# Two output products of a DiT layer: activations stationary, gates as rows, no transposition at the residual

## The chip, the core and the metric

The kernel runs on one core of one Trainium2 chip. The metric is the device time of one launch in microseconds (us). The kernel before took 1759.86 us in the median of three runs (1759.07 to 1762.25).

## The reference

The program computes two layers of a diffusion transformer on 512 latent tokens and 256 context tokens, 1024 channels wide, in f32. The change touches the first layer's two residual updates:

```python
a = rms_norm(h, norm1_g) * (1 + sc1) + sh1          # sc, sh, g: adaLN, from c
y = concat([y_conv, y_na], -1) @ w_out              # even mixer: convolution, neighbourhood attention
h = h + g1 * y                                      # g1: one gate per channel
t = rms_norm(h, norm2_g) * (1 + sc2) + sh2
h = h + g2 * ((silu(t @ w1) * (t @ w3)) @ w2)       # D_FF = 2816
# the same for the context tokens, with gates of their own
```

After them comes the second layer: an odd mixer (window attention and differential attention), and a mixture of eight experts. It is not touched.

## The kernel before, in words

All 768 tokens lie in `h` as six tiles of 128 tokens (partitions) by 1024 channels, f32: tiles 0 to 3 are the latents, 4 and 5 the context. Products are done in f16 with each f32 operand split in two (hi and lo) and three products for each 128 rows of the contraction: hi·hi, hi·lo, lo·hi. Activations for a product lie transposed, channels on partitions (`yT`, `gT`, `aT`), in both halves.

Weights are streamed by `Stream`: a block of up to 1 MB goes by DMA to one of two staging slots (`wst`), ACT casts the hi half (L282), DVE computes the lo half (L283). Two blocks are fetched ahead. Between the weight blocks lie the blocks `adr` of the adaLN matrix of later steps; each costs DVE four multiply-and-sum instructions of 128x1024 (L384, `adjk`).

The output projection of the first mixer (in `layer0`, L1042 to L1070, tiles `eops`) uses `mm1`: the weights of 128 output channels (one of eight `d`) are stationary, 512 columns of latent tokens (part 0) or 256 of context (part 1) move past. So the result is transposed, channels on partitions, and `resid` (L468) brings it back: ACT evicts it and multiplies by the gate, which is one number per partition (L474, `yT`), TensorE transposes it in 128x128 pieces, four in part 0 and two in part 1 (L477, `ytp`), DVE adds it to `h` (L479). After d = 4, 6 and 7 ACT sums the squares of what has been added (L465). The second product of the feed-forward (`ffn`, tiles `f` from `gT`, 22 contraction steps) is built in the same way, and also stores the four latent tiles of `h` to DRAM (`h_spill`, L1135).

Both products are followed by an RMS norm (`norm_steps`), one for the latents and one for the context. It sums the partial squares (L488), takes a reciprocal square root in small DVE steps (L330 to L342), scales the rows (L430 on DVE, L428 on ACT, tile `n`, or `h` in place), and then takes eight steps, one for each 128 channels: four transposes on PE (L440, `nps`), scale and shift on ACT (L447, `af`), hi and lo halves on DVE (L452, L453). The steps of the latents' norm are put between the matmuls of the last part 1, as many to a `d` as `NSTEP1` and `NSTEP2` say; the product that follows (`f` from `yT` after the projection, `pscq` after the feed-forward) needs them. The Tile framework sets the order of the instructions on each engine; each engine runs its queue in order.

`mm2` (L354) is the other form of a product, used in the next layer: 128 tokens of activations are stationary, up to 512 columns of weights move, and the result has tokens on partitions.

Of the kernel before, what the change touches and what calls it, by code (L numbers as in the profile page):

```python
# [50 lines left out]
NSTEP1 = (0, 2, 3, 3)  # L51
NSTEP2 = ((), (), (1, 3, 5, 7, 9), (0, 2, 4))
# [17 lines left out]
SSQ = {4: (0, 0), 6: (1, 5), 7: (2, 7)}  # L70

# [59 lines left out]
def layouts(i):  # L131
# [18 lines left out]
    A['w_evo'] = _pairs(_m1(f('ev_w_out')[0]))  # L150
    t1, t3 = _m1(f('ffn_w1')[0]), _m1(f('ffn_w3')[0])
    A['w_f13'] = _pairs(np.stack([t1, t3], 1).reshape(44, 128, 8, 128))
    A['w_f2'] = _w2(f('ffn_w2')[0])
# [161 lines left out]
class K:  # L315
# [168 lines left out]

    def ssq_sum(self, pool, ssq, part):
        t0, nt, mc = PARTS[part]
        ss = self.small.tile([128, nt], F32, name="sst", tag=f"sst{nt}", bufs=2)
        self.nc.vector.tensor_reduce(out=ss, in_=ssq[:, t0:t0 + nt, :], axis=AX.X, op=OP.add)  # L488
        return ss


    def blocks(self):
# [53 lines left out]
    def setup(self, ctx):  # L546
# [22 lines left out]
        self.adab = [cols[:, 0:48], cols[:, 48:96]]  # L569
        self.ada_o = ada_order()  # L570
# [371 lines left out]
    def conv_gemm(self, a, yT, cp, pp):  # L942
# [25 lines left out]
        for c in range(0, 4, 2):  # L968
# [29 lines left out]
            w = block()  # L998
            for ci in range(2):
# [11 lines left out]
    def layer0(self):  # L1011
# [30 lines left out]
        with ExitStack() as c:  # L1042
            rp = c.enter_context(tc.tile_pool(name="ro0", bufs=1))
            pp = c.enter_context(tc.tile_pool(name="po0", bufs=1, space=PSUM))
            def gemm(w, d, part):
                s0, sn = CHUNKS[part]
                ps = pp.tile([128, 512], F32, name=f"eops{d}_{part}", tag="m", bufs=4)
                for k in range(KD):
                    self.mm1(ps, w[0][:, d % 2], w[1][:, d % 2], k, yT[:, 0, :, s0:s0 + sn], yT[:, 1, :, s0:s0 + sn],
                             [(0, sn)], k == 0, k == 7)  # L1050
                self.resid(d, part, ps, 0, rp, pp, "tp", ssq=self.ssq)

            self.ssq = self.small.tile([128, 6, 3], F32, name="ssq1", tag="ssq", bufs=2)
            norm = None
            for d0 in (0, 2, 4):
                ws = []
                for j in ((d0 // 2,) if d0 < 4 else (2, 3)):
                    w = self.S.get(('evo', j))
                    ws.append([z.rearrange("p (j k c) -> p j k c", j=2, k=8) for z in w])
                for part in range(2):  # L1060
                    for d in range(d0, d0 + 2 * len(ws)):
                        if norm is None and d0 == 4 and part == 1:

                            norm = self.norm_steps(1, 0, self.h, self.ssq, yT, rp, pp, "n")
                            next(norm)
                        gemm(ws[(d - d0) // 2], d, part)
                        for _ in range(NSTEP1[d - 4] if norm is not None else 0):
                            next(norm, None)
            for _ in norm:
# [4 lines left out]
    def ffn(self):  # L1074
        nc, tc = self.nc, self.tc
        a = self.a1
        with ExitStack() as c:
# [25 lines left out]
            self.ssq = self.small.tile([128, 6, 3], F32, name="ssq2", tag="ssq", bufs=2)  # L1103
            self.hd = self.dram.tile([4, 128, D], F32, name="h_spill")
            for ds in ((0,), (1,), (2,), (3,), (4,), (5,), (6, 7)):
                ws = [[z.rearrange("p (k c) -> p k c", k=11) for z in self.S.get(('f2', 2 * d + s))]
                      for d in ds for s in range(2)]
                if ds == (6, 7):
                    self.spill(0, 6)
                for part, (s0, sn) in enumerate(CHUNKS):  # L1110
                    if ds == (6, 7) and part:

                        self.spill(6, 8)
                        a = self.a2 = self.big.tile([128, 2, KD, NT], F16, name="aT2", tag="A")
                        norm = self.norm_steps(2, 0, self.h, self.ssq, a, fp, pp, "ad", natural=True, inplace=True, aftag="gf")
                        next(norm)
                    for d in ds:
                        ps = pp.tile([128, 512], F32, name=f"f2_{d}_{part}", tag="m", bufs=6)
                        for s in range(2):
                            wh, wl = ws[2 * (d - ds[0]) + s]  # L1120
                            for k in range(11):
                                self.mm1(ps, wh, wl, k, gT[:, 0, :, s0:s0 + sn], gT[:, 1, :, s0:s0 + sn], [(0, sn)],
                                         s == 0 and k == 0, s == 1 and k == 10, kk=11 * s + k)
                                if ds == (6, 7) and part and k in NSTEP2[2 * (d - 6) + s]:
                                    next(norm, None)
# [1019 lines left out]
```

## Time and profile before

| | |
|---|---|
| median of the runs | 1759.86 us |
| profiled execution, own time | 1761.97 us |
| its span | 1760.1 us |
| its mean granted TensorE clock | 0.983 |
| output projection, first `eops` to first `f` matmul | 310.92 to 388.33 us |
| feed-forward's first product | 388.33 to 735.92 us |
| feed-forward's second product, to first `pscq` matmul | 735.92 to 925.06 us |

The profile is of one execution; its times stand in microseconds from the start of the span. PE is TensorE, PEld its weight loads, DVE is VectorE, ACT is ScalarE. A group's line gives line number, engine, operation, output and inputs with shapes, and the count; a busy PE counts the whole pipeline depth of each matmul, so the distance from one start to the next (the pitch) is what a stream of them costs, not their duration.

### The profile page before, as it was taken

To read this page: it belongs to the slowest core of one execution; us is meant where nothing else is said; L and a number is where in the kernel's file an instruction comes from. 1 tells how busy PE (TensorE), PEld (TensorE's weight loads), DVE (VectorE), ACT (ScalarE), POOL (GpSimd) and SP (SyncE) were. 2 spreads that over 40 slices of the span, in tenths; PEclk is the share of its full clock that TensorE was granted. 3 is DMA by queue.
4 is the path that set the end of the run, shared out by engine and by line. 5 is a ranking of instruction groups with operands and counts; after the bars stand their busy time and mean duration, and the time that the engine had idled before them with its cause. 6 is when DMAs were issued, how large, how long until landed. Compare 5 with 4: busy or idle time off the path is not lost. (4 is left out here: it accounts for less than half of the span.)

```text
span 1760.1 us, 36123 instructions
## 1 busy us (share of the span) xinstructions
PE 1651.1 (94%) x15124; PEld 1160.4 (66%) x15124; DVE 1235.6 (70%) x2388; ACT 887.5 (50%) x1436; POOL 141.3 (8%) x100
## 2 busy tenths in 40 slices
PE   4999999999999999999998999988789999999996
PEld 2455566556556666566555466457689988999996
DVE  7775989777654544333148999696797688788883
ACT  7754554253222221111244667564666577786773
POOL 0000000000000000000000000352130001010211
PEclk9999999999999999999999999999889999999998
DMA  8412432633443332233312201112658889999892
GB/s 340 149 63 100 156 109 97 243 117 120 144 144 137 127 144 97 74 114 114 117 61 81 96 1 61 44 43 77 232 179 314 258 281 359 337 338 359 301 327 65
DMA packets 53736, 286.83 MB, mean 163 GB/s; under 512 B 7760, under 2 KB 12880, under 8 KB 29504
## 3 DMA queue, kind: packets, MB, share of 16 engines
q1 hardware_dynamic: 47472, 272.78, 42.8%
q0 software_dynamic: 5232, 10.96, 2.9%
q8 instruction: 120, 1.97, 0.4%
q10 hardware_dynamic: 864, 0.72, 0.1%
q14 instruction: 48, 0.39, 0.1%
HBM read 272.57 MB, written 11.08 MB: 161 GB/s over the span
## 5 line engine op out<-in xcount | busy, mean ns | idle before, releaser
L351 PEld LDWEIGHTS <-whi 128*128 128x128 f16 x5120 | 464.5, 98 | 185.4 <-issue 11.5
L351 PE MATMUL f<-yT,whi 128*128 128x512 f16 (+1 forms) x1408 | 326.8, 327 | 1.5 <-ACT af L447 1.5
L351 PEld LDWEIGHTS <-wlo 128*128 128x128 f16 x2560 | 251.5, 98 | 90.0 <-issue 2.6
L283 DVE SCALAR_TENSOR_TENSOR wlo<-wst,whi 128x2048 f16<-128x2048 f32 (+2 forms) x134 | 214.6, 1612 | 60.4 <-ACT whi L282 60.3
L351 PE MATMUL f<-yT,wlo 128*128 128x512 f16 (+1 forms) x704 | 229.9, 327 | 0.0
L282 ACT ACTIVATE whi<-wst 128x2048 f16<-128x2048 f32 (+2 forms) x134 | 179.1, 1354 | 99.9 <-PE f L351 72.0
L384 DVE SCALAR_TENSOR_TENSOR adjk<-wst,srow 128x1024 bf16<-128x1024 f32 x96 | 117.3, 1222 | 98.0 <-DMA wst<-in_w_adr_dram 97.0
L351 PE MATMUL f<-gT,whi 128*128 128x512 f16 (+1 forms) x704 | 164.4, 326 | 0.0
L351 PEld LDWEIGHTS <-aT 128*128 128x128 f16 x2376 | 153.7, 98 | 2.9 <-issue 2.4
L351 PE MATMUL mps<-xT,whi 128*128 128x176 f16 (+6 forms) x1408 | 141.1, 227 | 1.1 <-DVE xT L1871 0.7
L351 PE MATMUL mps<-xT,wlo 128*128 128x176 f16 (+6 forms) x704 | 135.7, 227 | 0.0
L351 PE MATMUL f<-gT,wlo 128*128 128x512 f16 (+1 forms) x352 | 114.7, 326 | 0.0
L351 PE MATMUL mps<-xT,aT 128*128 128x112 f16 (+6 forms) x1584 | 105.8, 225 | 0.2 <-issue 0.2
L479 DVE TENSOR_TENSOR h<-h,ytp 128x256 f32<-128x256 f32 (+1 forms) x48 | 24.3, 506 | 112.1 <-PE ytp L477 111.8
L351 PE MATMUL cvps<-aT,whi 128*128 128x512 f16 (+1 forms) x384 | 84.0, 332 | 2.8 <-ACT Kl L646 2.3
L1101 ACT CAST gT<-g 128x512 f16<-128x512 f32 (+1 forms) x23 | 14.0, 608 | 130.8 <-DVE g L1098 130.8
L351 PE MATMUL mps<-mgT,whi 128*128 128x176 f16 (+6 forms) x704 | 72.1, 227 | 1.4 <-DVE mgf L1890 0.9
L351 PE MATMUL mps<-mgT,wlo 128*128 128x176 f16 (+6 forms) x352 | 68.2, 227 | 0.0
L1096 ACT ACTIVATE s<-f 128x512 f32<-128x512 f32 (+1 forms) x44 | 21.5, 489 | 84.0 <-PE f L351 83.9
L358 PEld LDWEIGHTS <-aT 128*128 128x128 f16 x384 | 37.4, 99 | 39.4 <-DVE aT L453 6.5
L351 PE MATMUL eops<-yT,whi 128*128 128x512 f16 (+1 forms) x256 | 61.2, 326 | 1.1 <-DVE yc L1002 1.1
L1098 DVE SCALAR_TENSOR_TENSOR g<-f,s 128x512 f32<-128x512 f32 (+1 forms) x44 | 24.4, 556 | 52.3 <-PE f L351 52.3
(420 smaller groups left out, 3470.8 us busy)
## 6 DMA issues: line engine op xcount, KB each, us to landing
wst<-in_w_adr_dram SPq DMA_DIRECT2D x32, 1024.0 KB, 4.8
wst<-in_w_m_dram SPq DMA_DIRECT2D x26, 1024.0 KB, 6.3
Kd<-in_w_m_dram SPq DMA_DIRECT2D x25, 1024.0 KB, 8.3
h<-in_w_m_dram SPq DMA_DIRECT2D x24, 1024.0 KB, 10.1
wst<-in_w_f_dram SPq DMA_DIRECT2D x22, 1024.0 KB, 4.9
Kd<-in_w_m_dram SPq DMA_DIRECT2D x19, 704.0 KB, 5.8
Qc<-in_w_m_dram SPq DMA_DIRECT2D x13, 1024.0 KB, 6.3
wst<-in_w_m_dram SPq DMA_DIRECT2D x18, 704.0 KB, 6.5
```

What stands on the lines that cost most here:

```text
L282: nc.scalar.activation(h, x, AF.Copy, scale=self.scale)
L283: nc.vector.scalar_tensor_tensor(out=l, in0=x, scalar=SW, in1=h, op0=OP.mult, op1=OP.subtract)
L351: mm(ps[:, s0:s0 + sn], w[:, k, :], a[:, kk, s0:s0 + sn], start=first and p == 0, stop=last and p == 2)
L358: mm(ps, al[:, kk, t0:t0 + 128], wh[:, k, :], start=False, stop=last)
L384: nc.vector.scalar_tensor_tensor(out=jk, in0=st[:, j * D:(j + 1) * D], scalar=1.0, in1=self.srow[:, t, :], op0=OP.mult, op1=OP.mult, accum ...
L479: nc.vector.tensor_tensor(out=hs, in0=hs, in1=tp[:, 0:w].rearrange("p (t c) -> p t c", t=nt), op=OP.add)
L1096: nc.scalar.activation(s[:, 0:sn], p[0][:, 0:sn], AF.Silu, scale=DESC)
L1098: nc.vector.scalar_tensor_tensor(out=g[:, 0:sn], in0=p[1][:, 0:sn], scalar=DESC * SA, in1=s[:, 0:sn], op0=OP.mult, op1=OP.mult)
L1101: nc.any.tensor_copy(gh, g[:, 0:sn])
```

## The change

Both products change to the form of `mm2`. The 1024 output channels are done in two halves of 512; in each half the six token tiles t come in turn, with 128 tokens stationary and 512 columns of weights moving. The result has tokens on partitions, as `h` has, and `resid_rows` needs no transposition: DVE multiplies the PSUM tile by the gates, adds the product to `h`, and ACT sums the squares of each half tile. A gate is now a number per column, so it is wanted as a row on all partitions: `gate_send` transposes the gates on TensorE and stores them to DRAM once per product, `gate_rows` reads a half of them to 128 partitions by DMA (`grow`, 128x2x512, one buffer). The weights of both products are laid out anew by halves; the second product of the feed-forward has 12 blocks in place of 16. Steps of the latents' norm stand after every second contraction step of the last two token tiles of half 1. The spill is four DMAs of half a tile's channels after t = 3 of each half.

```diff
--- before.py
+++ after.py
@@ -69,6 +67,8 @@
 PARTS = [(0, 4, 0), (4, 2, 1), (0, 2, 0), (2, 2, 0)]
 SSQ = {4: (0, 0), 6: (1, 5), 7: (2, 7)}
 
+F2K = (3, 3, 4, 4, 4, 4)
+
 
 
 def _perm():
@@ -482,6 +489,35 @@
             for t in range(t0, t0 + nt):
                 self.sumsq(pool, self.h, ssq[:, t, c:c + 1], t, c0 * 128, (dt + 1) * 128)
 
+    def gate_send(self, gi, pool, pspool, tag, bufs=2):
+
+        nc = self.nc
+        tp = pspool.tile([128, 512], F32, name=f"gtp{gi}", tag=tag, bufs=bufs)
+        gc = pool.tile([128, 16], F32, name="gc16", tag="gc16", bufs=1)
+        nc.vector.tensor_copy(gc.rearrange("p (t k) -> p t k", t=2), self.gate[gi].rearrange("p k t -> p t k"))
+        nc.tensor.transpose(tp[0:16, 0:128], gc, self.ident)
+        r = pool.tile([16, 128], F32, name="grow16", tag="grow16", bufs=1)
+        nc.vector.tensor_copy(r, tp[0:16, 0:128])
+        self.gd[gi] = self.dram.tile([16, 128], F32, name=f"gate_d{gi}")
+        nc.sync.dma_start(out=self.gd[gi], in_=r)
+
+    def gate_rows(self, gi, half, pool):
+
+        g = pool.tile([128, 2, 512], F32, name=f"grow{gi}_{half}", tag="grow", bufs=1)
+        v = self.gd[gi].rearrange("a c -> (a c)")
+        src = bass.AP(tensor=v.tensor, offset=v.offset + 512 * half, ap=[[0, 128], [D, 2], [1, 512]])
+        self.nc.sync.dma_start(out=g, in_=src)
+        return g
+
+    def resid_rows(self, t, half, ps, g, pool, ssq, tag="yT", bufs=2):
+
+        V = self.nc.vector
+        c = slice(512 * half, 512 * half + 512)
+        y = pool.tile([128, 512], F32, name=f"yg{t}_{half}", tag=tag, bufs=bufs)
+        V.tensor_tensor(out=y, in0=ps, in1=g[:, t // 4, :], op=OP.mult)
+        V.tensor_tensor(out=self.h[:, t, c], in0=self.h[:, t, c], in1=y, op=OP.add)
+        self.sumsq(pool, self.h, ssq[:, t, half:half + 1], t, 512 * half, 512 * half + 512)
+
     def ssq_sum(self, pool, ssq, part):
         t0, nt, mc = PARTS[part]
         ss = self.small.tile([128, nt], F32, name="sst", tag=f"sst{nt}", bufs=2)
@@ -515,8 +551,10 @@
             add(('cv', j), 'w_cv', j)
             for b in range(8 + 2 * j, min(10 + 2 * j, ADV)):
                 ada(0, b)
+        def rows(key, name, half, k0, n):
+            o.append((key, A[name][half][:, 512 * k0:512 * (k0 + n)], 512 * n))
         for j in range(4):
-            add(('evo', j), 'w_evo', j)
+            rows(('evo', j), 'w_evo', j // 2, 4 * (j % 2), 4)
             ada(0, ADV + j)
         rest = [(0, b) for b in range(20, 24)] + [(1, b) for b in range(24)]
         n = 0
@@ -996,6 +1035,8 @@
                     post.pop(0)()
                     yield 0.8
             w = block()
+            if c:
+                self.gate_send(0, cp, pp, "PT")
             for ci in range(2):
                 ps = yield from gemm(w, ci)
                 yc = cp.tile([128, NT], F32, name="yc", tag="yc", bufs=1)
@@ -1042,30 +1083,22 @@
         with ExitStack() as c:
             rp = c.enter_context(tc.tile_pool(name="ro0", bufs=1))
             pp = c.enter_context(tc.tile_pool(name="po0", bufs=1, space=PSUM))
...
+            self.ssq = self.small.tile([128, 6, 3], F32, name="ssq1", tag="ssq", bufs=2)[:, :, 0:2]
             norm = None
...
+            for half in range(2):
+                grow = self.gate_rows(0, half, rp)
+                ws = [[z.rearrange("p (k c) -> p k c", k=4) for z in self.S.get(('evo', 2 * half + j))] for j in range(2)]
+                for t in range(6):
+                    if half and t == 4:
+
+                        norm = self.norm_steps(1, 0, self.h, self.ssq, yT, rp, pp, "n")
+                        next(norm)
+                    ps = pp.tile([128, 512], F32, name=f"eops{half}_{t}", tag="m", bufs=4)
+                    for k in range(KD):
+                        self.mm2(ps, *ws[k // 4], k % 4, yT[:, 0], yT[:, 1], k, t * 128, k == 0, k == 7)
+                        if norm is not None and k % 2:
                             next(norm, None)
+                    self.resid_rows(t, half, ps, grow, rp, self.ssq)
             for _ in norm:
                 pass
         self.dump('h1', self.h)
@@ -1082,6 +1115,8 @@
             next(norm)
             for f in range(22):
                 w = [z.rearrange("p (j k c) -> p j k c", j=2, k=8) for z in self.S.get(('f13', f))]
+                if f == 6:
+                    self.gate_send(1, fp, pp, "ad")
                 for part, (s0, sn) in enumerate(CHUNKS):
                     p = []
                     for i in range(2):
@@ -1100,30 +1135,39 @@
                     gh, gl = (gT[:, z, f, s0:s0 + sn] for z in range(2))
                     nc.any.tensor_copy(gh, g[:, 0:sn])
                     nc.vector.tensor_tensor(out=gl, in0=g[:, 0:sn], in1=gh, op=OP.subtract)
...
+            self.ssq = self.small.tile([128, 6, 3], F32, name="ssq2", tag="ssq", bufs=2)[:, :, 0:2]
             self.hd = self.dram.tile([4, 128, D], F32, name="h_spill")
...
+            norm = None
+            for half in range(2):
+                grow = self.gate_rows(1, half, fp)
+                ps = [pp.tile([128, 512], F32, name=f"f2_{half}_{t}", tag="m", bufs=6) for t in range(6)]
+
+                def gemm(t, ws):
+                    for w, k0, n in ws:
+                        for k in range(n):
+                            kk = k0 + k
+                            self.mm2(ps[t], *w, k, gT[:, 0], gT[:, 1], kk, t * 128, kk == 0, kk == 21)
+                            if norm is not None and kk % 2:
+                                next(norm, None)
+                    if ws[-1][1] + ws[-1][2] == 22:
+                        self.resid_rows(t, half, ps[t], grow, fp, self.ssq, "s", 3)
+                        if t == 3:
+                            self.spill(4 * half, 4 * half + 4)
+                k0, ws = 0, []
+                for j, n in enumerate(F2K):
+                    w = [z.rearrange("p (k c) -> p k c", k=n) for z in self.S.get(('f2', 6 * half + j))]
+                    ws.append((w, k0, n))
+                    k0 += n
+
+                    if j == 4:
+                        continue
+                    for t in range(6):
+                        if half and j == 5 and t == 4:
+                            a = self.a2 = self.big.tile([128, 2, KD, NT], F16, name="aT2", tag="A")
+                            norm = self.norm_steps(2, 0, self.h, self.ssq, a, fp, pp, "ad", natural=True, inplace=True, aftag="gf")
+                            next(norm)
+                        gemm(t, ws)
+                    ws = []
             for _ in norm:
                 pass
         self.dump('h2', self.h)
```

DVE's queue at the end of the output projection, before: `ytp_7_0` is the last transposed result of the latents, `ssq` and `sst` the sums of squares, `rs_*` the reciprocal square root, `n_0` the normalised tile.

```order
L479 TENSOR_TENSOR h<-h,ytp_7_0_4388 128x4x128 [waits PE_49]
L488 TENSOR_REDUCE sst<-ssq_3906 128x4 [waits Activation_49]
L330 TENSOR_SCALAR rs_v<-sst 128x4 [waits DVE_49]
L331 TENSOR_SCALAR rs_r<-rs_v 128x4 [waits DVE_49]
L340 TENSOR_TENSOR rs_t<-rs_r 128x4 [waits DVE_49]
L341 SCALAR_TENSOR_TENSOR rs_t<-rs_t,rs_v 128x4 [waits DVE_49]
L479 TENSOR_TENSOR h<-h,ytp_4_1_4450 128x2x128 [waits PE_49]
L342 SCALAR_TENSOR_TENSOR rs_r<-rs_t,rs_r 128x4 [waits DVE_49]
```

And now: `yg_1` is the product with the gates of half 1, `eops_3` and `eops_4` the results of token tiles 3 and 4, `adjk` the adaLN instructions.

```order
L517 TENSOR_TENSOR yg_1_4297<-eops_3_4272,grow_1_4139 128x512 [waits PE_49]
L518 TENSOR_TENSOR h<-h,yg_1_4297 128x512 [waits DVE_49]
L391 SCALAR_TENSOR_TENSOR adjk,adred<-wst_4496,srow 128x1024 [waits DMAHW1_49]
L524 TENSOR_REDUCE sst<-ssq_3914 128x4 [waits Activation_49]
L391 SCALAR_TENSOR_TENSOR adjk,adred<-wst_4496,srow 128x1024 [waits DVE_49]
L337 TENSOR_SCALAR rs_v<-sst 128x4 [waits DVE_49]
L391 SCALAR_TENSOR_TENSOR adjk,adred<-wst_4496,srow 128x1024 [waits DVE_49]
L338 TENSOR_SCALAR rs_r<-rs_v 128x4 [waits DVE_49]
L517 TENSOR_TENSOR yg_1_4384<-eops_4_4323,grow_1_4139 128x512 [waits PE_49]
L347 TENSOR_TENSOR rs_t<-rs_r 128x4 [waits DVE_49]
L391 SCALAR_TENSOR_TENSOR adjk,adred<-wst_4496,srow 128x1024
L348 SCALAR_TENSOR_TENSOR rs_t<-rs_t,rs_v 128x4 [waits DVE_49]
```

Four `adjk` instructions and the multiplication for tile 4 now stand in the chain from the last addition of the latents to `n_0`; before, only one addition of a context piece stood there.

PE's queue where the latents' norm begins, before: `eops_1` tiles are of part 1 (context), `nps` are the norm's transposes.

```order
L351 LDWEIGHTS whi_4071
L351 MATMUL eops_1_4507<-yT_1586,whi_4071 128x256
L351 LDWEIGHTS wlo_4072
L351 MATMUL eops_1_4507<-yT_1586,wlo_4072 128x256
L351 LDWEIGHTS whi_4071
L351 MATMUL eops_1_4507<-yT_1586,whi_4071 128x256
L440 MATMUL nps_0_4489<-ident,n_0_4418 128x128 [waits DVE_49]
L440 MATMUL nps_1_4498<-ident,n_0_4418 128x128
L351 LDWEIGHTS whi_4071
L351 MATMUL eops_1_4507<-yT_1586,whi_4071 128x256
L351 LDWEIGHTS wlo_4072
L351 MATMUL eops_1_4507<-yT_1586,wlo_4072 128x256
```

And now, in token tile 5 of half 1, the last of the projection:

```order
L365 LDWEIGHTS yT_1586
L365 MATMUL eops_5_4389<-whi_3953,yT_1586 128x512
L447 MATMUL nps_0_4330<-ident,n_0_4318 128x128 [waits DVE_49]
L447 MATMUL nps_1_4345<-ident,n_0_4318 128x128
L363 LDWEIGHTS yT_1586
L363 MATMUL eops_5_4389<-whi_3953,yT_1586 128x512
L364 LDWEIGHTS yT_1586
L364 MATMUL eops_5_4389<-wlo_3954,yT_1586 128x512
L447 MATMUL nps_0_4330<-ident,n_0_4318 128x128 [waits DVE_49]
L447 MATMUL nps_0_4330<-ident,n_0_4318 128x128 [waits Activation_49]
L447 MATMUL nps_1_4345<-ident,n_0_4318 128x128 x2
L365 LDWEIGHTS yT_1586
```

Before, the first `nps` came after four matmuls of d = 6's part 1, with 44 of 256 columns still to come; now it comes in tile 5, after seven of its eight contraction steps, with three of 512 columns still to come.

SP's queue at the projection's start, now: `gate_d` is the store of the gates, `grow_0` the rows of half 0, `wst` blocks of weights and of adaLN, `h` the loads of the residual.

```order
L266 DMA wst_3603<-in_w_adr_dram 128x2048 [waits DMAHW6_49,DMAHW5_49,DVE_49]
L266 DMA wst_3609<-in_w_evo_dram 128x2048 [waits DMAHW4_49,DVE_49]
L502 DMA gate_d_3617<-grow_3615 16x128 [waits DMAHW0_49,DVE_49]
L509 DMA grow_0_3915<-gate_d_3617 128x2x512 [waits DMAHW0_49,PE_49]
L266 DMA wst_3930<-in_w_adr_dram 128x2048 [waits DMAHW6_49,DVE_49]
L1082 DMA h<-in_x_dram 128x1024 [waits PE_49]
L1082 DMA h<-in_x_dram 128x1024 x3
```

The two new DMAs stand ahead of an adaLN block and of the six loads of `h`, which followed directly upon the third weight block and that adaLN block before.

## Rows read from the trace of the kernel before

**Rows 1.** Part 1 of the page: busy time, share, instructions of each engine.
```profile
PE 1651.1 (94%) x15124; PEld 1160.4 (66%) x15124; DVE 1235.6 (70%) x2388; ACT 887.5 (50%) x1436; POOL 141.3 (8%) x100
```

**Rows 2.** Windows: start:end, length, busy time by engine, PEclk, DMA share, GB/s.
```profile
310.92:388.33 77.41, 74.68 (x464) 45.52 (x464) 57.41 (x116) 34.64 (x70) 0.00 (x0) 1.00 0.48 179
388.33:395.20 6.87, 6.87 (x25) 2.79 (x25) 6.87 (x19) 1.27 (x4) 0.00 (x0) 0.75 0.63 229
395.20:735.92 340.72, 340.56 (x2105) 205.78 (x2104) 180.63 (x346) 79.01 (x97) 0.00 (x0) 1.00 0.36 126
735.92:925.06 189.14, 184.56 (x1139) 110.98 (x1137) 60.27 (x103) 50.54 (x87) 0.00 (x0) 1.00 0.28 98
```

**Rows 3.** PE's timeline in the next stage, whose activations are stationary.
```profile
928.11 0.38 PE L358 MATMUL pscq<-whi,aT 128*128 128x512 f16 x1
...
930.91 0.38 PE L356 MATMUL pscq<-whi,aT 128*128 128x512 f16 x1
```

**Rows 4.** PE's timeline about a set of transposes: start, length, instruction, count.
```profile
368.99 0.38 PE L351 MATMUL eops<-yT,whi 128*128 128x256 f16 x2
...
369.65 0.27 PE L351 MATMUL eops<-yT,whi 128*128 128x256 f16 x1
369.94 0.66 PE L477 MATMUL ytp<-ident,yT 128*128 128x128 f32 x4
370.43 0.27 PE L351 MATMUL eops<-yT,whi 128*128 128x256 f16 x1
```

**Rows 5.** Line groups in 310.92:388.33: shapes, count, busy us, mean ns, idle before.
```profile
L384 DVE SCALAR_TENSOR_TENSOR adjk<-wst,srow 128x1024 bf16<-128x1024 f32 x20 | 24.5, 1223 | 3.4 <-DMA wst<-in_w_adr_dram 3.1
...
L477 PE MATMUL ytp<-ident,yT 128*128 128x128 f32 x48 | 8.6, 289 | 0.7 <-ACT yT L474 0.3
...
L447 ACT ACTIVATE af<-nps,nB,nA 128x512 f32<-128x512 f32 x8 | 6.0, 772 | 0.0
...
L479 DVE TENSOR_TENSOR h<-h,ytp 128x512 f32<-128x512 f32 x8 | 5.5, 687 | 8.4 <-PE ytp L477 8.3
...
L453 DVE TENSOR_TENSOR yT<-af,yT 128x512 f16<-128x512 f32 x7 | 4.5, 685 | 0.0
...
L465 ACT ACTIVATE sqj<-h 128x640 bf16<-128x640 f32 x6 | 4.4, 736 | 2.7 <-DVE h L479 1.5 <-issue 1.1
...
L479 DVE TENSOR_TENSOR h<-h,ytp 128x256 f32<-128x256 f32 x8 | 3.3, 416 | 2.6 <-PE ytp L477 2.6
...
L452 DVE CAST yT<-af 128x512 f16<-128x512 f32 x7 | 2.8, 422 | 0.0
```

**Rows 6.** DVE's timeline, from the latents' last addition to the first normalised tile.
```profile
370.63 0.69 DVE L479 TENSOR_TENSOR h<-h,ytp 128x512 f32<-128x512 f32 x1 [3.35 <-PE ytp L477]
373.15 0.17 DVE L488 TENSOR_REDUCE sst<-ssq 128x4 f32<-128x12 f32 x1 [1.83 <-ACT sqj L465]
...
375.74 1.42 DVE L430 TENSOR_SCALAR n<-h,rs_r 128x1024 f32<-128x1024 f32 x2
```

**Rows 7.** PE's wait at the feed-forward's start, window 310.92:400.
```profile
PE f L351 <- ACT af L447: 1.5, 1, 1.5
```

**Rows 8.** PE's timeline, the second product's first matmul after its last latent piece.
```profile
900.49 0.38 PE L351 MATMUL f<-gT,whi 128*128 128x256 f16 x2
```

**Rows 9.** PE's waits in 735.92:940: line, waited for, total, times, longest.
```profile
PE nps L440 <- DVE h L430: 2.6, 1, 2.6
PE ytp L477 <- ACT yT L474: 2.2, 2, 1.4
PE pscq L356 <- DVE h L479: 2.0, 1, 2.0
```

**Rows 10.** DMA issues of the page: instruction, count, KB each, median us to landing.
```profile
h<-in_x_dram SPq DMA_DIRECT2D x6, 512.0 KB, 7.8
...
h_spill<-h SPq DMA_DIRECT2D x4, 384.0 KB, 4.4
```

**Rows 11.** Tile h: all its DMAs, issue to landing.
```profile
DMA to landing us min/median/max: 1.8/6.5/28.7
```

More of the change, by code (lines that the diff above doesn't have):

```diff
@@ L49 @@
 NDIF = 4
-NSTEP1 = (0, 2, 3, 3)
-NSTEP2 = ((), (), (1, 3, 5, 7, 9), (0, 2, 4))
 NSTEP3 = 4
@@ L95, in _m2, with _halves @@
     return np.ascontiguousarray(t.reshape(128, 2, 4, n).transpose(1, 0, 2, 3)).reshape(2, 128, -1)
+def _halves(w):
+    k, n = w.shape
+    t = w.reshape(k // 128, 128, 2, n // 2).transpose(2, 1, 0, 3)
+    return np.ascontiguousarray(t).reshape(2, 128, -1)
 def _w2(w):
@@ L149, in layouts @@
     A['w_qkv'] = np.concatenate([_m2(ev[:, 1536 + 512 * j:2048 + 512 * j]) for j in range(3)], 0)
-    A['w_evo'] = _pairs(_m1(f('ev_w_out')[0]))
+    A['w_evo'] = _halves(f('ev_w_out')[0])
     t1, t3 = _m1(f('ffn_w1')[0]), _m1(f('ffn_w3')[0])
     A['w_f13'] = _pairs(np.stack([t1, t3], 1).reshape(44, 128, 8, 128))
-    A['w_f2'] = _w2(f('ffn_w2')[0])
+    A['w_f2'] = _halves(f('ffn_w2')[0])
     od = f('od_w_in')[0]
@@ L526, in blocks @@
             n += 1
-        for j in range(16):
-            add(('f2', j), 'w_f2', j)
-            if j % 2 == 1 and n < len(rest):
+        for j in range(12):
+            rows(('f2', j), 'w_f2', j // 6, sum(F2K[:j % 6]), F2K[j % 6])
+            if j % 2 == 0:
                 ada(*rest[n])
@@ L569, in setup @@
         self.adab = [cols[:, 0:48], cols[:, 48:96]]
+        self.gd = {}
         self.ada_o = ada_order()
@@ L1044, in layer0 @@
             pp = c.enter_context(tc.tile_pool(name="po0", bufs=1, space=PSUM))
[L1045 to L1053, printed above, removed]
-            norm = None
[L1055 to L1067, printed above, removed]
+            self.ssq = self.small.tile([128, 6, 3], F32, name="ssq1", tag="ssq", bufs=2)[:, :, 0:2]
+            norm = None
+            for half in range(2):
[9 more added lines that the diff above has]
+                        if norm is not None and k % 2:
                             next(norm, None)
+                    self.resid_rows(t, half, ps, grow, rp, self.ssq)
             for _ in norm:
@@ L1102, in ffn @@
                     nc.vector.tensor_tensor(out=gl, in0=g[:, 0:sn], in1=gh, op=OP.subtract)
-            self.ssq = self.small.tile([128, 6, 3], F32, name="ssq2", tag="ssq", bufs=2)
+            self.ssq = self.small.tile([128, 6, 3], F32, name="ssq2", tag="ssq", bufs=2)[:, :, 0:2]
             self.hd = self.dram.tile([4, 128, D], F32, name="h_spill")
[L1105 to L1125, printed above, removed]
-                        self.resid(d, part, ps, 1, fp, pp, "ad", ssq=self.ssq)
```

## The prediction

> **What bounds the kernel now.** I read the page's first part first: TensorE is busy for 94% of the span, VectorE for 70% [rows 1]. That share is an average, so I then cut the span at the borders of the two changed products [rows 2]. In the output projection PE works 74.68 of 77.41 us, in the second product 184.56 of 189.14, and in the feed-forward's first product between them 340.56 of 340.72. So PE's queue is the clock of all three stretches: an instruction that leaves PE shortens the time, provided that no wait takes its place, and a stage that starts earlier passes its gain on whole through the stretch between. DVE works 57.41 of 77.41 us in the projection (74%) but 60.27 of 189.14 in the second product (32%): the first has little room for more DVE work, the second has much. Granted clock is 1.00 in all but the first 6.87 us of the feed-forward, where 0.75 is a mixture of the two levels 1.2 and 2.4 GHz, after the idle time at the end of the projection.
>
> **What a matmul and a transposition cost.** In a stream whose activations are stationary, 13 matmuls of 512 columns start in 930.91 - 928.11 = 2.80 us, 0.2154 each [rows 3]; that is the form which both products take. One of 256 columns is (369.65 - 368.99)/6 = 0.110 [rows 4]. Two of 256 thus cost 0.22, against 0.2154 for one of 512. A set of four transposes costs 370.43 - 369.65 - 0.11 = 0.67 us of PE's time, 0.18 of it a gap [rows 4]; a set of two I put at half. Each product has 8 sets of four and 8 of two: 8 x 0.67 + 8 x 0.33 = 8.0 us. Their summed durations, 8.6 us for 48 [rows 5], are more than the 0.11 us between two starts would make of them (5.3), for they overlap.
>
> The Trainium skill ("TensorE: Matmul & The Clock Gate", section "Part 4: PE-mode transpose") puts a 128x128 transpose at about 275 ns inside a kernel. The mean duration here, 289 ns, agrees, but the starts are closer. By that figure as a cost, an estimate of 96 x 0.275 = 26 us would go in place of my 16; that result is the fourth rival below.
>
> **The output projection.** Matmuls before: 8 d x 8 steps x 3 = 192 of 512 columns and 192 of 256, so 41.4 + 21.1 = 62.5 us. After: 2 halves x 6 tiles x 24 = 288 of 512, 62.0 us. The products themselves give 0.5.
> Up to the last matmul of latent tokens, before took 368.99 - 310.92 = 58.07 us [rows 2, 4]. After, latent tile 3 of half 1 is matmul 240, so 51.7 us, with nothing else in PE's queue until then. Gain to this point: 6.4.
> From there the latents' norm decides. Before, 388.33 - 368.99 = 19.34 us went by until the feed-forward began, of which the norm's chain on DVE was 375.74 - 370.63 = 5.1 to the first scaled tile [rows 6], behind 44 matmuls of cover. After, the chain starts on DVE with two passes of 512 columns (0.69 each) [rows 5], and holds four adaLN instructions of 1.22 [rows 5] and tile 4's two passes (1.4), which the trace of before doesn't have there. Sum on DVE: 0.2 + 1.4 + 4.9 + 1.4 + 11 small steps at 0.2 (373.15 to 375.74 [rows 6], less the addition in it) 2.2 + three more of about 0.17, 0.5 = 10.6 us; the square sums on ACT, 0.74 and its readout [rows 5], lie beside the first adaLN instruction. First scaled tile at 11.3, last of three on DVE at 12.7. PE reaches the first norm transposition after 45 matmuls, 9.7 us: it waits from 1.6 to 3. Six of the eight steps then have no matmul to lie beside, and go at ACT's 0.77 us each [rows 5], some 0.1 less where they overlap: 12.7 + 0.6 + 8 x 0.75 = 19.3. So the tail is as long as before, 19.3 against 19.34, in spite of 5 us fewer of PE work in it.
> Two further losses come behind it. The context's norm waits for tile 5, whose addition is in DVE's queue behind all eight steps' halves (0.42 + 0.69 each [rows 5]); it comes to its first transposition 37 matmuls after the feed-forward's start in place of 44, and I count 2.3 us for the wait. PE's idle tail is longer by about 5 us of missing matmuls; before, after a wait of 1.5 us [rows 7] and transposes, 25 matmuls took 6.87 us where they would take 5.4 at the full clock [rows 2]. I add 1 for it. Net: 6.4 - 2.3 - 1 = 3 us, between -1 (DVE late by 4 more) and 7 (neither loss comes).
> Rather than by matmuls, this is a trade on DVE: 8 x 0.687 + 8 x 0.416 = 8.8 us of additions become 24 x 0.69 = 16.5 [rows 5]. In 72 us, 57.4 + 7.7 = 65 are then busy.
>
> **The second product.** Before: 22 x 3 x 8 = 528 of 512 columns and 528 of 256: 113.7 + 58.1 = 171.8 of 189.14. After: 792 of 512, 170.6. To the last latent piece before: 900.49 - 735.92 = 164.57 [rows 2, 8]; after, 744 matmuls, 160.3. Gain 4.3.
> The tail before is 925.06 - 900.49 = 24.6 us: 132 matmuls of 256 columns (14.5), 32 norm transposes (3.5), sets of transposes, and waits of 2.2 on ACT for the piece to be transposed and 2.0 on DVE for the last addition [rows 9]. After it, DVE's chain is 0.2 + 1.4 + 0.9 (squares) + 2.2 = 4.7, scaled tiles until 6.8; no adaLN block stands in it. PE arrives after 23 matmuls, 4.95: it waits 1.9. Then DVE sets the pace: tile 4's passes 1.4, eight steps at about 1.0, tile 5's 1.4, some weight halves. That ends at 17.5, against the 10.3 of matmuls and 3.5 of transposes that PE has. The spill, four of 256 KB, lands in 2 to 4 us by its neighbours [rows 10], before the third scaled tile overwrites `h`. Gain in the tail 24.6 - 17.5 = 7.1; together 11.4, between 8 and 14. DVE's extra 7.7 us lies in 129 idle ones.
>
> **The rest.** Two gate stores, two small transposes and four copies: 0.5 us at most on PE and DVE; below zero nothing, since no work goes. Four row loads of 512 KB have 7.8 us as their nearest row [rows 10], and a late one is the third rival. The weight stream carries the same bytes. Sum: 3 + 11.4 - 0.5 = 13.9 us. The profiled execution's own time is 1761.97 (span 1760.1), so 1748.1; the median of the runs is 2.1 lower, 1759.86, and I forecast 1746.
>
> **Rivals.**
> 1. The tails cost nothing: scaled tiles are in time, both norms are hidden. Then the projection keeps 6.4 and the second product reaches 170.6 + 3.5 + 1 = 175, a gain of 14: -20, 1740. For it: DVE could have done its adaLN work earlier than I think. Against it: the order has them in the chain.
> 2. DVE becomes the bound at both ends: 4 us more at the projection (net -1), 3 at the second product (8): -7, 1753. For it: 65 of 72 us busy. Against it: DVE has idle time before the third tile in both.
> 3. Slower: the gate rows of half 1 come late in the projection. `grow` has one buffer, so the load can start only when half 0's last multiplication is done, 31 us + 0.9 after the stage's start, behind other loads in SP's queue. Half 1's first tile wants it at 31 + 5.2; four PSUM tiles let PE go on until 51.7, so a landing within 15 us costs little, and later ones cost what they are late, with DVE's queue blocked behind the multiplication. Nearest rows: 7.8 us, longest of any load or store of `h` 28.7 [rows 10, 11]. At 28.7 it costs about 14, all of the gain; beyond 30 us the kernel is slower, and at 36 us it takes 1767. In the second product the same load has all six tiles' first 14 steps, 54 us, as cover.
> 4. Each transposition is worth its duration: 96 x 0.289 [rows 5] = 27.7, 1732. Rows 4 speak against it.
> 5. No change: PE's freed time turns into waits for weights at the next block. Against it: PE's first product is busy for 99.95% [rows 2].
>
> **How the numbers follow.** Forecast 0.65, rival 1 0.13, 2 0.11, 3 0.04, 4 0.02, 5 0.05. The range reaches from rival 1 to rival 2 with a little beyond each: 1739 to 1755. 0.2% of the time is 3.5 us, about what a measurement of this kernel tells from no change. Faster: forecast and rivals 1, 2 and 4, less 0.02 for rival 2's slow end, 0.89; same: rival 5 and that end, 0.07; slower: rival 3, 0.04.
>
> **What the profile after would show.** Matmuls at 0.2154 in both products, no `ytp` in them; the projection's first `f` matmul some 71 us after its first `eops`, and `pscq` 178 us after the second product's first `f`; PE waiting 1.6 to 3 us for `n` and 2 for `h`; at both ends a low PE share for 7 us. The prediction is wrong in the size of the tails if those windows differ by more than 4 us, wrong in the cost of a transposition if the stretch to tile 3 isn't 51.7 or 160.3 us, and wrong in kind if PE waits for `grow` or weights.

## The result and the profile after

The changed kernel took 1739.83 us in the median of four runs (1737.98 to 1741.19), the kernel before 1760.3 beside it: a ratio of 0.9882, 95% interval 0.9865 to 0.9899. That is 20.5 us faster. The forecast was 1746 with 1739 to 1755: the right side, and inside the range only just, at its lower end; the gain forecast was 6 us short.

The profiled execution took 1740.66 us, its span 1738.9 (before 1761.97 and 1760.1). Its windows, cut at the same borders as [rows 2], with one more behind them, up to the first `psdk` matmul:

```profile
311.02:384.34 73.32, 67.38 (x321) 31.35 (x321) 60.75 (x120) 24.95 (x43) 0.00 (x0) 1.00 0.51 192
384.34:390.40 6.06, 6.06 (x21) 2.44 (x21) 6.06 (x15) 1.19 (x3) 0.00 (x0) 0.72 0.24 61
384.34:731.75 347.41, 347.41 (x2129) 208.63 (x2129) 190.91 (x369) 80.08 (x100) 0.00 (x0) 1.00 0.39 134
731.75:908.80 177.05, 175.29 (x826) 80.81 (x824) 63.80 (x102) 38.09 (x54) 0.00 (x0) 1.00 0.29 101
908.80:983.83 75.03, 67.44 (x423) 37.90 (x424) 68.40 (x227) 43.23 (x92) 7.41 (x15) 1.00 0.23 78
```

The projection takes 73.32 us in place of 77.41, the feed-forward's first product 347.41 as against 347.59 (6.87 + 340.72), the second product 177.05 in place of 189.14. PE has 321 matmul records in the projection where it had 464. The last window is one that the forecast never looked at; before it was this:

```profile
925.06:1003.20 78.14, 69.64 (x432) 39.18 (x432) 68.99 (x222) 43.29 (x93) 6.48 (x15) 0.98 0.23 80
```

It is 3.1 us shorter too. Together: 4.1 + 0.2 + 12.1 + 3.1 = 19.5 of the 21.2 us between the two spans. The rest lies in later stages. The first `eops` itself started anywhere from 306.8 to 312.0 us in the profiled executions below, though nothing ahead of it differs but the gates' way to DRAM. The granted clock up to there (the number behind the five busy times) goes with it: 1.00 in the three that start by 307.7 (`f2_only`, `evo_only`, `add_tp`), 0.98 or 0.99 in the seven that start from 310.2 on. Here are `f2_only` and before:

```profile
0.00:306.82 306.82, 277.20 (x2312) 164.28 (x2313) 251.16 (x530) 176.56 (x283) 6.77 (x12) 1.00 0.41 146
```

```profile
0.00:310.92 310.92, 280.22 (x2312) 165.14 (x2313) 251.40 (x529) 176.75 (x283) 6.76 (x12) 0.99 0.40 144
```

So totals of single executions differ by some microseconds that have nothing to do with an edit, and stages are compared window by window.

PE's waits in the projection and at its end, then at the second product's end (waiter, waited for, total, times, longest):

```profile
PE nps L447 <- DVE n L437: 2.5, 1, 2.5
PE nps L447 <- ACT af L454: 2.1, 4, 0.9
PE f L358 <- ACT af L454: 1.3, 1, 1.3
```

```profile
PE nps L447 <- DVE h L437: 0.6, 1, 0.6
PE pscq L363 <- DVE yg L517: 1.1, 1, 1.1
```

PE waits 2.5 us for the scaled tile in the projection, as foreseen. At the second product's end it waits 0.6 for the scaled tile, where the sum had 1.9, and 1.1 at the first `pscq`, where before it waited 2.2 for ACT's evicted tile and 2.0 for DVE's last addition [rows 9]. DVE's timeline tells why the projection's is the longer. First the chain there, from latent tile 3's multiplication on, which answers to [rows 6]:

```profile
363.02 0.69 DVE L517 TENSOR_TENSOR yg<-eops,grow 128x512 f32<-128x512 f32 x1 [0.56 <-PE eops L365]
363.74 0.69 DVE L518 TENSOR_TENSOR h<-h,yg 128x512 f32<-128x512 f32 x1
366.69 1.22 DVE L391 SCALAR_TENSOR_TENSOR adjk<-wst,srow 128x1024 bf16<-128x1024 f32 x1 [2.26 <-DMA wst<-in_w_adr_dram]
367.85 0.15 DVE L524 TENSOR_REDUCE sst<-ssq 128x4 f32<-128x8 f32 x1
...
374.33 0.75 DVE L437 TENSOR_SCALAR n<-h,rs_r 128x1024 f32<-128x1024 f32 x1
```

And the same chain at the second product's end:

```profile
892.53 0.69 DVE L517 TENSOR_TENSOR yg<-f,grow 128x512 f32<-128x512 f32 x1 [3.76 <-PE f L365]
893.26 0.69 DVE L518 TENSOR_TENSOR h<-h,yg 128x512 f32<-128x512 f32 x1
894.80 0.16 DVE L524 TENSOR_REDUCE sst<-ssq 128x4 f32<-128x8 f32 x1 [0.85 <-ACT sqj L472]
...
897.17 1.42 DVE L437 TENSOR_SCALAR h<-h,rs_r 128x1024 f32<-128x1024 f32 x2
```

From the multiplication to the first scaled tile it takes 11.3 us in the projection and 4.6 in the second product. The difference lies in the four adaLN instructions, tile 4's two passes, and the 2.26 us for which DVE stood idle from 364.4 because the first adaLN instruction waited for its block: `sst` was behind it in the queue, though its squares were done at 365.25. Behind the scaled tiles come ACT's eight steps, and casts of weights among them; these are the two groups in the projection's tail, 362.70 to 384.33 (count, then busy us and mean ns):

```profile
L454 ACT ACTIVATE af<-nps,nB,nA 128x512 f32<-128x512 f32 x8 | 6.0, 770 | 0.0
L289 ACT ACTIVATE whi<-wst 128x512 f16<-128x512 f32 x8 | 4.7, 617 | 0.0
```

### The profile page after: what moved, and what is told of

Read it like the earlier page. It is cut to its first block, busy times and chain, and to the rows that moved or that the text cites. A ratio compares the mean times of both kernels' runs of the same rounds, so it can differ in the third digit from the quotient of the medians.

```text
span 1738.9 us, 35145 instructions
## 1 busy us (share of the span) xinstructions
PE 1630.4 (94%) x14670; PEld 1115.0 (64%) x14670; DVE 1246.9 (72%) x2405; ACT 865.1 (50%) x1375; POOL 143.7 (8%) x100
## 5 line engine op out<-in xcount | busy, mean ns | idle before, releaser
L358 PEld LDWEIGHTS <-whi 128*128 128x128 f16 x4160 | 370.6, 98 | 124.9 <-issue 12.2
L290 DVE SCALAR_TENSOR_TENSOR wlo<-wst,whi 128x2048 f16<-128x2048 f32 (+3 forms) x130 | 213.8, 1654 | 90.0 <-ACT whi L289 89.8
L289 ACT ACTIVATE whi<-wst 128x2048 f16<-128x2048 f32 (+3 forms) x130 | 178.0, 1388 | 148.9 <-PE f L365 77.5
L358 PEld LDWEIGHTS <-wlo 128*128 128x128 f16 x2080 | 204.5, 98 | 60.4 <-issue 2.5
L358 PEld LDWEIGHTS <-aT 128*128 128x128 f16 x2376 | 153.7, 98 | 2.7 <-issue 2.2
L363 PE MATMUL f<-whi,gT 128*128 128x512 f16 x264 | 100.1, 379 | 0.0
L364 PE MATMUL f<-wlo,gT 128*128 128x512 f16 x264 | 100.1, 379 | 0.0
L365 PE MATMUL f<-whi,gT 128*128 128x512 f16 x264 | 100.1, 379 | 0.0
L472 ACT ACTIVATE sqj<-h 128x512 bf16<-128x512 f32 (+3 forms) x36 | 20.9, 582 | 98.0 <-DVE h L518 59.6
L365 PEld LDWEIGHTS <-aT 128*128 128x128 f16 x384 | 37.1, 98 | 38.4 <-DVE aT L460 6.5
L363 PEld LDWEIGHTS <-aT 128*128 128x128 f16 x384 | 37.6, 99 | 36.6 <-ACT aT L457 5.1
L364 PEld LDWEIGHTS <-aT 128*128 128x128 f16 x384 | 37.5, 98 | 30.8 <-issue 3.4
```

What stands on the lines that cost most here:

```text
L289: nc.scalar.activation(h, x, AF.Copy, scale=self.scale)
L290: nc.vector.scalar_tensor_tensor(out=l, in0=x, scalar=SW, in1=h, op0=OP.mult, op1=OP.subtract)
L358: mm(ps[:, s0:s0 + sn], w[:, k, :], a[:, kk, s0:s0 + sn], start=first and p == 0, stop=last and p == 2)
L363: mm(ps, ah[:, kk, t0:t0 + 128], wh[:, k, :], start=first, stop=False)
L364: mm(ps, ah[:, kk, t0:t0 + 128], wl[:, k, :], start=False, stop=False)
L365: mm(ps, al[:, kk, t0:t0 + 128], wh[:, k, :], start=False, stop=last)
```

## The experiments

All were timed against the kernel before, in two sets; before had a median of 1760.3 us in both. The last four rows are the second set, in which the changed kernel did not run, so they are held against it by way of before. The windows are those above, in each kernel's own profile.

| us | projection | second product | pscq to psdk | median |
|---|---|---|---|---|
| before | 77.41 | 189.14 | 78.14 | 1760.3 |
| changed | 73.32 | 177.05 | 75.03 | 1739.83 |
| changed, again | 72.43 | 177.05 | 75.06 | 1740.68 |
| evo_only | 72.36 | 189.12 | 80.58 | 1753.36 |
| f2_only | 77.40 | 177.05 | 75.20 | 1744.15 |
| adr_late | 68.27 | 177.06 | 75.05 | 1736.70 |
| no_ytp | 71.71 | 178.22 | 79.12 | - |
| add_tp | 78.60 | 181.97 | 79.96 | 1758.05 |
| no_mult | 71.04 | 177.05 | 77.93 | - |
| masks_pool | 77.41 | 189.13 | 76.12 | 1756.64 |

`no_ytp` and `no_mult` compute other values, and what follows the router takes some 2100 us in place of 501 (medians 3344.48 and 3344.70), which fits tokens that go to other experts. Their totals say nothing, and only their windows ahead of it are read.

**The changed kernel again.** 

> The changed kernel again, on the same chip as the three others: 20 us faster than the kernel before, 1740.

1740.68 us, ratio 0.9891 (0.9875 to 0.9906): as expected. The projection's window differs by 0.9 between its two profiles, which is the least that a difference there must exceed.

**Each half of the change alone.** `evo_only` has the old second product, `f2_only` the old projection, each with its weights' old layout and without the other's gate store:

```diff
+            for ds in ((0,), (1,), (2,), (3,), (4,), (5,), (6, 7)):   # evo_only: the old loop
...
-            self.gate_send(0, cp, pp, "PT")                           # f2_only: no gate rows for the projection
```

> Only the output projection is changed; the second product of the feed-forward is as before. Theory (the stages add up): the projection's window, first eops to first f matmul, is 73.3 us as in the full change, everything behind as before, so 4 us faster than the kernel before. Rival 1 (the later gain behind the feed-forward, 4.9 us after the first pscq, comes from the shift in time of the whole program and not from the second product): 8 to 9 us faster. Rival 2 (the projection's gain is lost at its end, as the forecast's losses had it): 0 to 2 us faster.

> Only the second product of the feed-forward is changed. Theory (the stages add up, and the 4.9 us gained behind the first pscq come from how the second product ends): second product 177 us, stage of pscq to psdk 75.0 in place of 78.1, in all 17 us faster than the kernel before. Rival (the gain behind the first pscq is the shift's): 12 us faster, pscq to psdk 78.

```profile
307.48:379.84 72.36, 67.37 (x320) 31.34 (x320) 60.68 (x120) 24.95 (x43) 0.00 (x0) 1.00 0.52 196
915.42:996.00 80.58, 70.68 (x432) 39.75 (x431) 68.86 (x222) 43.32 (x93) 6.48 (x15) 0.96 0.22 77
```

```profile
731.34:908.39 177.05, 175.30 (x826) 80.78 (x824) 63.82 (x102) 38.08 (x54) 0.00 (x0) 1.00 0.29 101
908.39:983.59 75.20, 67.44 (x423) 37.86 (x424) 68.57 (x227) 43.24 (x92) 7.58 (x15) 1.00 0.23 77
```

`f2_only` is 16.2 us faster (ratio 0.9911, 0.9896 to 0.9926), and its stage behind the first `pscq` takes 75.20, as in the full change. `evo_only` is 6.9 us faster (0.9962, 0.9948 to 0.9977), more than the 4 expected. The interval reaches from 4 to 9 us, so the total can't tell the theory's 4 from rival 1's 8 to 9; the stage can. Behind the first `pscq` it is no shorter than before, but longer (80.58, at a granted clock of 0.96 where before had 0.98). So that gain comes with the second product, and a shift of the program alone doesn't bring it. 16.2 + 6.9 is 23.1 against the 19.6 of both in the same set, which the intervals allow.

**What the transposes cost.** `no_ytp` is the kernel before with the transposes of `resid` left out; `add_tp` is the changed one with as many idle ones put in:

```diff
-        for t in range(nt):
-            nc.tensor.transpose(tp[:, t * 128:(t + 1) * 128], y[:, t * 128:(t + 1) * 128], self.ident)
...
+        if part < 2:                                                  # no_ytp: the two products' parts
+            tp = y
...
+        for j in range(4):                                            # add_tp, in resid_rows
+            self.nc.tensor.transpose(tp[:, j * 128:(j + 1) * 128], self.ident, self.ident)
```

> The kernel before without the 96 PE transposes at the two residuals: DVE adds ACT's evicted tile as it stands, so the result is left untransposed; everything else of before stays. Theory (in place, a set costs what the stream shows, 0.67 us for four with its gap and half of that for two): 16 us faster than the kernel before, 1744; the projection's stretch to the last latent matmul 52 us in place of 58.1. Rival 1 (a transposition costs only its pitch of 0.107 us): 10 us faster. Rival 2 (its duration of 0.289): 27 us faster.

> The changed kernel with four idle transposes of 128x128 f32 put behind each of the 24 result tiles (96 in all, of the identity, into a PSUM tile that nobody reads). They wait for nothing, so there is no gap. Theory (pitch without a gap, 0.107 us): 8 to 10 us slower than the changed kernel, some of the last ones hidden in the tails' waits. Rival 1 (a set costs 0.67 us even so, because of the change of form in the stream): 16 us slower. Rival 2 (duration): 27 us slower.

```profile
312.03:383.74 71.71, 66.79 (x416) 40.75 (x416) 56.64 (x115) 34.80 (x70) 0.00 (x0) 1.00 0.52 193
731.50:909.72 178.22, 176.13 (x1090) 106.52 (x1088) 58.38 (x99) 49.07 (x84) 0.00 (x0) 1.00 0.30 104
```

Without its transposes the old form loses 77.41 - 71.71 = 5.7 us in the projection and 189.14 - 178.22 = 10.9 in the second product: 16.6, where the sum had 16.0. The projection's stretch to the last latent matmul is 51.9 us, as expected. Idle ones, put into the new form, cost what PE's starts say:

```profile
318.48 0.60 PE L521 MATMUL xtra<-ident 128*128 128x128 f32 x4
318.92 0.38 PE L363 MATMUL eops<-whi,yT 128*128 128x512 f16 x1
```

The next matmul starts 0.44 us after a set of four, 0.11 for each, which makes 10.5 us for 96, and the two windows grow by 5.3 to 6.2 and by 4.9 (in the first the granted clock was 0.98 in place of 1.00, by an estimate up to 1.6 of that may be the clock's). So of the 16.6 us some 10.5 were PE's own time and about 6 the gaps and waits for ACT's evicted tile that went with them. `add_tp` as a whole is 17.4 us slower than the changed kernel in place of 8 to 10: a miss. 4.9 of it lie behind the first `pscq`, where PE waits 4.4 us for `h` and the changed kernel 1.3 (the experiment with the loads, below, shows on what DVE waits there); 1.8 lie in the feed-forward's first product (349.16 against 347.41) and were not followed up.

The mean duration of a transposition is 0.289 us [rows 5]; by it 27 us would have gone. The figure of about 275 ns in the Trainium skill ("TensorE: Matmul & The Clock Gate", "Part 4: PE-mode transpose") is a duration, and the duration here agrees with it; as a price in a stream both runs here refute it.

**What DVE's passes cost.** `no_mult` is the changed kernel without the gates' multiplication:

```diff
-        V.tensor_tensor(out=y, in0=ps, in1=g[:, t // 4, :], op=OP.mult)
-        V.tensor_tensor(out=self.h[:, t, c], in0=self.h[:, t, c], in1=y, op=OP.add)
+        V.tensor_tensor(out=self.h[:, t, c], in0=self.h[:, t, c], in1=ps, op=OP.add)
```

> The changed kernel without the multiplication by the gates: one DVE pass per result tile in place of two, the rows are loaded and not used. Theory (DVE's extra passes are hidden except in the two norm chains): 2 to 3 us faster than the changed kernel, from 0.69 to 1.4 at each end. Rival (DVE's throughput bounds the projection): 6 to 8 us faster, all of it in the projection.

```profile
310.40:381.44 71.04, 66.99 (x321) 31.23 (x320) 54.66 (x110) 24.76 (x44) 0.00 (x0) 1.00 0.51 191
728.97:906.02 177.05, 175.30 (x826) 80.72 (x824) 56.93 (x92) 38.35 (x54) 0.00 (x0) 1.00 0.28 98
```

The projection gains 1.4 to 2.3 us, the second product nothing (177.05 in all three profiles): the extra passes are hidden there, at its end too, where 0.69 or more was expected. DVE isn't the projection's bound by throughput either. Its total can't be read, and the 2.9 us that it loses behind `pscq` are again a matter of the loads (the next but one experiment) and of the granted clock, 0.98 in that stage in place of 1.00.

**The adaLN blocks at the projection's end.** `adr_late` moves three adaLN blocks behind later weights, and with them the second product's gate store by three steps:

```diff
             add(('f13', j), 'w_f13', j)
-            ada(*rest[n])
-            n += 1
+            if j > 2:
+                ada(*rest[n])
+                n += 1
...
-            if j % 2 == 0:
+            if j % 2 == 0 or j < 6:
...
-                if f == 6:
+                if f == 9:
                     self.gate_send(1, fp, pp, "ad")
```

> The full change, but three adaLN blocks (those behind the first three weight blocks of the feed-forward) are moved behind later blocks, so that DVE's queue at the projection's end holds no adjk between the last latent addition and the scaled tiles. Theory (DVE's chain sets the projection's end): the first f matmul comes 16 to 17 us after the last matmul of latent tile 3, as at the second product's end, in place of 21.5, so 4 to 5 us faster than the full change (1735). Rival 1 (ACT's eight steps and the low clock set it): under 1.5 us. Rival 2 (the blocks moved into the feed-forward delay its weights): slower than the full change.

```profile
310.21:378.48 68.27, 66.59 (x321) 31.37 (x320) 47.05 (x87) 23.94 (x41) 0.00 (x0) 1.00 0.42 160
378.48:725.09 346.61, 345.87 (x2130) 208.24 (x2130) 203.59 (x395) 81.59 (x101) 0.00 (x0) 1.00 0.40 140
```

```profile
362.21 0.69 DVE L517 TENSOR_TENSOR yg<-eops,grow 128x512 f32<-128x512 f32 x1 [3.76 <-PE eops L365]
362.94 0.69 DVE L518 TENSOR_TENSOR h<-h,yg 128x512 f32<-128x512 f32 x1
364.48 0.16 DVE L524 TENSOR_REDUCE sst<-ssq 128x4 f32<-128x8 f32 x1 [0.85 <-ACT sqj L472]
...
366.85 0.75 DVE L437 TENSOR_SCALAR n<-h,rs_r 128x1024 f32<-128x1024 f32 x1
```

```profile
PE f L358 <- DVE yg L517: 1.1, 1, 1.1
PE nps L447 <- DVE n L437: 0.5, 1, 0.5
```

The chain is now the second product's, 4.6 us, PE waits 0.5 in place of 2.5 for the scaled tile, and the first `f` matmul comes 16.6 us after tile 3's last matmul (310.21 + 51.7 = 361.9). The window shrinks by 4.2 to 5.0 us, and neither product behind it, whose streams take the moved blocks, is longer (346.61 and 177.06). The two lines above are all that PE waits at the projection's end, 1.6 us in place of 5.9; the waits for ACT's steps are gone with DVE's, so rival 1 is refuted. The edit takes more off DVE than the block in the chain (it is busy for 47.05 us in place of 60.75), but PE waited for DVE and ACT nowhere else in the window. In all 1736.70 us (1734.56 to 1737.52), ratio 0.9867 (0.9849 to 0.9885) to before; the changed kernel beside it had 1740.68 (1739.94 to 1742.30). This is the fastest version.

**The gain behind the first pscq.** The stage differs in the order of two loads. Before, SP issued a weight block, then ACT the constants, and DVE's queue, in which the cast of the constants (`masks`) stood ahead of the context's norm, waited for them:

```profile
925.67 0.33 SPq L259 DMA_DIRECT2D wst<-in_w_dq_dram  x1
```

```profile
925.90 0.34 ACTq L1142 DMA_DIRECT2D cst<-in_consts_dram  x1
```

```profile
930.98 0.29 DVE L1152 CAST masks<-cst 128x256 bf16<-128x256 f32 x1 [2.49 <-DMA cst<-in_consts_dram]
```

In the changed kernel the constants went first:

```profile
911.07 0.34 ACTq L1186 DMA_DIRECT2D cst<-in_consts_dram  x1
```

```profile
912.97 0.33 SPq L266 DMA_DIRECT2D wst<-in_w_dq_dram  x1
```

```profile
913.68 0.28 DVE L1196 CAST masks<-cst 128x256 bf16<-128x256 f32 x1
```

128 KB issued 0.23 us behind 1 MB were waited for until 5.1 us after their issue; issued 1.9 us ahead of it, they were there within 2.6. No run changes this order alone, but all ten profiles follow it. The casts wait 1.9 to 2.5 us in `before`, `evo_only`, `no_ytp` and `no_mult`, which have the block first (in `masks_pool`, which has it first too, they are no longer on DVE), and not at all in `after`, its repetition, `f2_only` and `adr_late`, which have the constants first. `add_tp` has both: its 128 KB went 0.49 us ahead of the block (919.68 and 920.17) and were not waited for, the last of the constants (`natf`, 2 KB) went 0.37 us behind it and was waited for until 6.8 us after its issue:

```profile
927.31 0.17 DVE L1598 CAST nat<-natf 128x4 int32<-128x4 f32 x1 [3.31 <-DMA natf<-in_consts_dram]
```

`masks_pool` is the kernel before with that cast, and a second of the same kind, on GpSimd:

```diff
-        nc.vector.tensor_copy(self.masks, cst.rearrange("p (s c) -> p s c", s=2))
+        nc.gpsimd.tensor_copy(self.masks, cst.rearrange("p (s c) -> p s c", s=2))
...
-                nc.vector.tensor_copy(self.nat, nf)
+                nc.gpsimd.tensor_copy(self.nat, nf)
```

> The kernel before with two small casts of constants (masks, nat) moved from DVE to GpSimd, so that the DMA of the constants no longer holds up the context's norm on DVE. Theory (that DMA wait is part of the 3.1 us which the stage from pscq to psdk lost in the changed kernel): that stage shrinks from 78.1 to 75.5 to 77, the wait of nps at its start from 2.6 to under 1.5. Rival (the stage is longer before only because its first seven matmuls run at the lower clock): 78, no change.

```profile
923.92:926.92 3.00, 3.00 (x10) 1.15 (x10) 3.00 (x13) 1.31 (x5) 0.00 (x0) 0.64 0.40 101
923.92:1000.04 76.12, 69.79 (x431) 39.42 (x431) 67.87 (x220) 43.13 (x93) 7.89 (x17) 0.98 0.23 81
```

The stage takes 76.12 in place of 78.14, PE no longer waits for `h` in it (2.6 before [rows 9]), and the total is 3.7 us lower, ratio 0.9984 (0.9969 to 0.9998). So the wait for the constants cost the kernel before 2.0 us. How much of the changed kernel's 3.1 us this is, the runs do not show, for at least three things differ there. PE still waits 1.3 us for `h` in it, so only 1.4 of the 2.6 went:

```profile
PE nps L447 <- DVE h L437: 1.3, 1, 1.3
```

Then the granted clock is 1.00 over the whole stage, in place of 0.98; 2% of 78 us, an estimate of 1.6 us at most. And the stage's border moved: nine small matmuls of the attention (`cS`, `PT`) that stood ahead of the first `psdk` now stand behind it (432 and 423 matmul records), at 0.11 us each an estimate of 1 us that is only shifted to the next stage. What PE did before the clock was low can be read from the first 3 us of the stage in before, in the changed kernel, and in `evo_only`, and from a later stretch of `evo_only`:

```profile
925.06:928.06 3.00, 3.00 (x8) 1.11 (x8) 3.00 (x13) 1.60 (x5) 0.00 (x0) 0.55 0.42 106
```

```profile
908.80:911.80 3.00, 3.00 (x14) 1.38 (x15) 3.00 (x9) 2.05 (x5) 0.00 (x0) 1.00 0.02 5
```

```profile
915.42:918.42 3.00, 3.00 (x14) 1.36 (x14) 3.00 (x13) 1.43 (x5) 0.00 (x0) 1.00 0.43 104
924.40:931.40 7.00, 5.33 (x15) 2.53 (x16) 4.07 (x12) 1.02 (x2) 0.00 (x0) 0.51 0.30 124
```

Before waited 2.0 us at the first `pscq` and then had 0.55 of the clock, `masks_pool` 2.0 and 0.64, the changed kernel 1.1 and 1.00. But `evo_only` waited 2.0 as well and had 1.00; there the clock fell to 0.51 at its wait of 4.0 us for `h`, which ends 10.6 us after the first `pscq` as in before, and that is why its stage is longer than before's. So the length of one wait alone doesn't decide, and what does stays open. The Trainium skill ("DMA: Bandwidth & Descriptors", "Issuing engines are not separate DMA queues") says that transfers run on the same 16 engines whichever engine issues them; the constants on ACT's queue that came late behind SP's block agree with it.

## Why the prediction was right, and where it was not

- **Transposes: right.** 16.0 us by the sets' price in the stream, 16.6 measured by `no_ytp`. The stretch to tile 3, 51.7 us, is right too: its result was multiplied at 363.02, 52.0 after the first `eops`.
- **The projection: mechanism right, size off twice.** 3 us were forecast, 4.1 to 5.0 came (73.32, 72.43). The tail from tile 3 took 21.6 us (384.34 - 362.7) where the sum had 19.3. The first scaled tile was done after 12.4 us (375.1) in place of 11.3: the first adaLN instruction waited 2.26 for its block, which the sum didn't have, and the rest of the chain took 1.2 less than counted. From there 9.3 us went by in place of 8.0: ACT's eight steps (`af`) take the 6.0 us that were counted, but casts of weights (`whi`) stand between them, so they spread over 7.3 (376.95 to 384.28). And the 3.3 us taken off for the context's norm and a longer stretch at the lower clock did not come. PE waits for nothing in the feed-forward's first product but the 1.3 at its start, and the stretch at the lower clock is as before: 21 matmuls in 6.06 us, 1.5 above full pitch, against 25 in 6.87, also 1.5 [rows 2]. The "5 us fewer of PE work" in the tail was a misreading: PE is busy for 16.9 us of before's tail and 15.7 of the new one.
- **The second product: right.** 11.4 forecast, 12.1 measured; 160.3 to the last latent matmul, then 16.7 in place of the 17.5 of the sum, with a wait of 0.6 for the scaled tile in place of 1.9.
- **The rest: the step that failed.** The sum ended at the first `pscq` and put all that is left at -0.5 us. There, 3.1 us were gained in the next stage and, in that one profile, 1.7 in the stages behind it. By what came of each term, the forecast was short by 1.1 in the projection, 0.7 in each of the two products of the feed-forward (the -0.5 is not to be seen in the first), 3.1, and 1.7. At least one part of this stood in the trace of before: the 2.6 us for which `nps` waits for `h` [rows 9] lie behind the first `pscq`, and the forecast never asked for what DVE waited there. That wait (1.4 of it went), the clock and the moved border make up the 3.1; their shares stay open. That the result lies inside the range is therefore luck in part.
- **The rivals.** Rival 1's number, 1740, is the time measured, but not by its way: the tails are not hidden, PE waits 5.9 us at the projection's end. What it took for hidden tails is made up by the gain behind the first `pscq` and the two losses that did not come, so its number fits by luck. Rival 2's 1753 is 13 us off, and `no_mult` shows that DVE's throughput is no bound (it is busy for 60.75 us of the projection, where 65 were counted); but `adr_late` shows that DVE's chain does set the projection's end. Rival 3 is refuted by DVE's one wait of 1.2 us for the gate rows, rival 4 by `no_ytp` and `add_tp`, rival 5 by 347.41 us of PE's work in 347.41.

## What to carry to other kernels

An instruction that PE runs in a stream cost the distance between starts plus the gap that its input leaves, and not its duration: 0.11 us and 0.17 with the gaps, at a duration of 0.29. When a bound engine is relieved, read the queue of the engine that the next stage waits for, up to the point where the two traces have the same distance again, and not only to the next stage's first matmul: side work that stands in a chain there (a block of adaLN, a cast that waits for a small load behind a large one) decides how much of the gain arrives, and moving it was worth 4 us here.

## What the runs showed of the hardware

A 128x128 f32 transposition took 0.11 us of PE's stream, though its record is 0.27 us or more long. A load of 128 KB issued on ACT's queue a quarter of a microsecond behind 1 MB on SP's was usable after 5.1 us; one that went ahead of it, after at most 2.6. In `add_tp` 2 KB issued 0.37 us behind such a block were usable after 6.8 us.
